# Attention on one Trainium2 core: queries and keys cast by the loading transfer, and 64-wide transposes in column tiles

## The chip, the cores and the metric

The kernel runs on one core of a Trainium2 chip. The time is the device time of one execution in microseconds (us), where lower is better. Several executions were timed of each version. The span is the length of one profiled execution on the chip, a little less than the timed one; the granted clock is the share of its full speed at which TensorE was let run. A run is called slow where it is over 1.5% above the fastest of the same kernel.

## The reference

```python
# q, k, v: float32, (batch 8, heads 8, seq 512, dim 64)
scale = 1.0 / np.sqrt(q.shape[-1])
scores = np.einsum('bhqd,bhkd->bhqk', q, k) * scale
scores = scores - scores.max(axis=-1, keepdims=True)
attn = np.exp(scores)
attn = attn / attn.sum(axis=-1, keepdims=True)
return np.einsum('bhqk,bhkd->bhqd', attn, v).astype(np.float32)
```

## The kernel before

The 64 heads are worked on as 32 pairs. A pair's queries and keys are loaded as fp32, cast to fp16, transposed on TensorE, and copied from PSUM by VectorE. TensorE then computes scores in blocks of 128 keys by 512 queries (a "unit", 256 in all), ScalarE takes the exponential of three units in one instruction, and TensorE multiplies by the values, with a column of ones for the sum. Eight units go through a polynomial on VectorE instead ("asides"). The order of all instructions is fixed when the kernel is built.

The parts that the change and the argument touch:

```python
def load(g, names="qkv"):                     # plain loads, on SyncE's queue
    ...
    for nm in names:
        r = lpool.tile([P, 2, NI * D], FP32, tag=f"{nm}32", name=f"{nm}32_{g}")   # 7 buffers a name
        nc.sync.dma_start(out=r, in_=rows(dict(q=q, k=k, v=v)[nm], g))
        raw[g, nm] = r

def cast_qk(g):                               # GpSimd: cast, and interleave the pair's two heads
    ...
    qk = xpool.tile([P, 2, NI, P], FP16, tag="qk", name=f"qk_{g}")
    for n in range(2):
        nc.gpsimd.tensor_copy(
            out=qk[:, n].rearrange("p i (h d) -> p i h d", d=D),
            in_=raw[g, "qk"[n]].rearrange("p h (i d) -> p i h d", d=D),
        )
    halves[g] = qk

def transpose(g, parts=(0, 1)):
    ...
    for n in parts:
        for i in range(NI):                   # 128-wide: both heads at once
            nc.tensor.transpose(ps[:, n - lo, i, :], halves[g][:, n, i, :], ident16)
    nc.vector.tensor_copy(out=turned[g][:, lo:hi], in_=ps)

# the opening
load_head(0, "q", nc.sync); load_head(0, "k", nc.scalar)      # pair 0 has its own path (both heads)
...
load(1, "qk")
load(0, "v")
for g in range(2, AHEAD):                     # AHEAD = 6
    load(g, "qk")
    load(g - 1, "v")
...
cast_qk(1); cast_v(0); cast_qk(2); cast_v(1)
# then, at the first unit of each pair g: cast_qk(g + 3), cast_v(g + 2), load(g + 6, "qk"), load(g + 5, "v")
```

The softmax here doesn't subtract the row's maximum and nothing guards it: scores larger than these inputs give would overflow.

## Time and profile before

| | before |
|---|---|
| median of the first three runs | 123.97 us (123.07 to 126.07) |
| profiled execution, span | 121.2 us |
| ScalarE busy | 113.9 us (94%) |
| exponentials: busy, and idle between them | 111.5 us, 0.8 us |
| GpSimd's casts of queries and keys | 62 instructions, 47.2 us |

The row to look at is ScalarE's. An engine that works without a pause from the opening to the close sets the end; the others matter only when they make it wait. The lines themselves are in the prediction.

### The profile page before, as it was taken

The numbers are of one execution on the slowest core, as the hardware profiler recorded it, in microseconds if no ns is written. First come the engines' busy times: TensorE is split into PE (matmuls) and PEld (weight loads), VectorE is DVE, ScalarE is ACT, GpSimd is POOL, SyncE is SP. The second block draws the span as 40 slices with busy tenths as digits, with TensorE's granted clock in tenths as the row PEclk, the third lists the DMA queues.
The fourth block names the chain that finished last, engine by engine and source line by source line (L and its number), as shares of the span: only waits on it lengthen the run. The fifth ranks groups of instructions, "written<-read, shape, count | busy, mean of one in ns | idle before, by whom it ended". The sixth has DMA issues, their size and how long they took to land.

```text
span 121.2 us, 4018 instructions
## 1 busy us (share of the span) xinstructions
PE 107.6 (89%) x1572; PEld 64.8 (53%) x1572; DVE 87.5 (72%) x213; ACT 113.9 (94%) x90; POOL 71.1 (59%) x109
## 2 busy tenths in 40 slices
PE   6989999898899998989988999899898998999680
PEld 6635646445564565456545656466455544666260
DVE  1342689979868985978787698766996899566170
ACT  4599999999999999999999999999999999999970
POOL 2188759869921992697199259990597099500000
PEclk9999999999999999999999999999999999999999
DMA  3999999999999999699999999999899895034213
GB/s 108 301 345 354 350 344 364 377 362 354 373 357 358 338 328 328 234 283 283 309 311 306 284 311 316 321 354 318 250 338 313 278 294 178 10 105 160 87 52 121
DMA packets 34882, 33.81 MB, mean 279 GB/s; under 512 B 2096, under 2 KB 34864, under 8 KB 34864
## 3 DMA queue, kind: packets, MB, share of 16 engines
q1 hardware_dynamic: 34576, 33.30, 84.6%
q10 hardware_dynamic: 288, 0.26, 0.7%
q8 instruction: 12, 0.20, 0.7%
q14 instruction: 6, 0.05, 0.1%
HBM read 25.17 MB, written 8.39 MB: 277 GB/s over the span
## 4 chain that ended last, share of the span: by engine, by line
ACT 74%; issue 15%; PE 5%; DMA 2%; DVE 1%
ACT pt L223 74%; DMA raw<-in_k_dram 2%; PE st L175 2%; PE o L234 1%; PE open L153 1%; DVE osb L248 1%; DVE rcp L247 0%; PE st L409 0%; DVE x L149 0%
## 5 line engine op out<-in xcount | busy, mean ns | idle before, releaser
L223 ACT ACTIVATE pt<-st 128x1536 f16<-128x1536 f32 (+2 forms) x85 | 111.5, 1609 | 0.8 <-PE st L175 0.8
L175 PE MATMUL st<-tqk 64*128 64x512 f16 x240 | 48.7, 380 | 7.0 <-ACT pt L223 5.9
L234 PEld LDWEIGHTS <-pt 128*128 128x128 f16 x992 | 33.8, 97 | 18.3 <-issue 12.4
L234 PE MATMUL o<-vp,pt 128*128 128x65 f16 x976 | 38.6, 194 | 0.9 <-DVE osb L248 0.3
L248 DVE TENSOR_TENSOR osb<-o,rcp 128x256 f32<-128x256 f32 x63 | 26.8, 425 | 2.2
L105 POOL CAST qk<-k 128x512 f16<-128x512 f32 x31 | 27.3, 880 | 0.6
L134 DVE COPY tqk<-tps 128x1024 f16<-128x1024 f16 (+1 forms) x32 | 21.2, 669 | 6.2 <-PE tps L133 5.9
L247 DVE RECIPROCAL rcp<-o 128x4 f32<-128x4 f32 x63 | 11.2, 178 | 17.4 <-PE o L234 17.1
L114 POOL CAST vp<-v 128x512 f16<-128x512 f32 x32 | 21.5, 672 | 2.6 <-DMA v<-in_v_dram 1.4
L105 POOL CAST qk<-q 128x512 f16<-128x512 f32 x31 | 19.9, 642 | 2.7 <-DMA q<-in_q_dram 1.8
L133 PEld LDWEIGHTS <-qk 128*128 128x128 f16 x248 | 14.2, 97 | 11.9 <-issue 4.5
L175 PEld LDWEIGHTS <-tqk 64*128 64x128 f16 x240 | 11.5, 93 | 15.8 <-issue 7.7
L133 PE MATMUL tps<-ident,qk 128*128 128x128 f16 x248 | 19.2, 220 | 0.7 <-DVE osb L248 0.3
L200 POOL TENSOR_SCALAR e<-n 128x512 int32<-128x512 int8 x8 | 5.0, 620 | 24.7 <-DVE n L197 24.6
L210 DVE SCALAR_TENSOR_TENSOR pa<-a,f 128x512 f16<-128x512 f32 x8 | 7.4, 930 | 0.0
L210 DVE SCALAR_TENSOR_TENSOR f<-f,e 128x512 f32<-128x512 f32 x8 | 6.9, 862 | 0.0
L210 DVE SCALAR_TENSOR_TENSOR a<-f 128x512 f32<-128x512 f32 x8 | 6.2, 771 | 0.0
L210 DVE SCALAR_TENSOR_TENSOR f<-sa,n 128x512 f32<-128x512 f32 x8 | 5.5, 692 | 0.3
L197 DVE TENSOR_SCALAR n<-sa 128x512 int8<-128x512 f32 x8 | 5.4, 681 | 0.0
L409 PE MATMUL warm<-blank 128*128 128x128 f16 x24 | 2.7, 313 | 1.0 <-DVE small L396 1.0
L234 PEld LDWEIGHTS <-pa 128*128 128x128 f16 x32 | 1.5, 97 | 3.6 <-DVE pa L210 1.7
L409 PEld LDWEIGHTS <-blank 128*128 128x128 f16 x28 | 2.7, 140 | 1.1 <-DVE small L396 1.0
(30 smaller groups left out, 20.4 us busy)
## 6 DMA issues: line engine op xcount, KB each, us to landing
v<-in_v_dram SPq DMA_DIRECT2D x32, 256.0 KB, 5.4
q<-in_q_dram SPq DMA_DIRECT2D x31, 256.0 KB, 5.1
k<-in_k_dram SPq DMA_DIRECT2D x31, 256.0 KB, 5.3
out_dram<-osb SPq DMA_DIRECT2D x31, 256.0 KB, 3.7
raw<-in_k_dram ACTq DMA_DIRECT2D x2, 128.0 KB, 2.9
raw<-in_q_dram SPq DMA_DIRECT2D x2, 128.0 KB, 2.7
out_dram<-osb SPq DMA_DIRECT2D x2, 128.0 KB, 1.7
```

Of the source, the lines that this page charges most:

```text
L105: nc.gpsimd.tensor_copy(out=qk[:, n].rearrange("p i (h d) -> p i h d", d=D), in_=raw[g, "qk"[n]].rearrange("p h (i d) -> p i h d", d=D),)
L114: nc.gpsimd.tensor_copy(out=vps[g % NV][:, :, :, 0:D], in_=raw[g, "v"].rearrange("p h (i d) -> p h i d", d=D),)
L133: nc.tensor.transpose(ps[:, n - lo, i, :], halves[g][:, n, i, :], ident16)
L134: nc.vector.tensor_copy(out=turned[g][:, lo:hi], in_=ps)
L175: nc.tensor.matmul(st[j][:, x, :], key, tq, start=True, stop=True)
L197: nc.vector.tensor_scalar(out=n, in0=s, scalar1=rate, scalar2=SHIFT, op0=AluOp.mult, op1=AluOp.add)
L210: nc.vector.scalar_tensor_tensor(out=o, in0=x, scalar=k, in1=y, op0=op0, op1=op1)
L223: nc.scalar.activation(out=pt[j][:, 0:n], in_=st[j][:, 0:n], func=EXP, scale=scale)
L234: nc.tensor.matmul(o[:, i, :], p[:, i * P : (i + 1) * P], vps[g % NV][:, h, c, :], start=(c == 0 and i == blocks[0]), stop=(c == NI - 1), ...
L247: nc.vector.reciprocal(out=rcp[:, lo:hi], in_=o[:, lo:hi, D:W])
L248: nc.vector.tensor_tensor(out=o_sb[g][:, h, lo:hi], in0=o[:, lo:hi, 0:D], in1=rcp[:, lo:hi].broadcast_to([P, hi - lo, D]), op=AluOp.mult,)
L409: nc.tensor.matmul(tile[:, G - 1, 0:P], blank, blank, start=True, stop=True)
```

## The change

Its intent is to take 47 us of casts from GpSimd. The transfer itself casts. The casting transfers are issued by GpSimd, so the loads of pairs 2 to 31 move from SyncE's queue to GpSimd's. Without a cast there is no interleave, so each head's 64 columns are transposed by themselves, into the upper or lower half of the PSUM tile's partitions.

```diff
+    def load_cast(g):
...
+        qk = xpool.tile([P, 2, 2, NI, D], FP16, tag="qk", name=f"qk_{g}", bufs=AHEAD + 4)
+        for n in range(2):
+            nc.gpsimd.dma_start(
+                out=qk[:, n].rearrange("p h i d -> p h (i d)"), in_=rows((q, k)[n], g)
+            )
+        halves[g] = qk
...
             for i in range(NI):
-                nc.tensor.transpose(ps[:, n - lo, i, :], halves[g][:, n, i, :], ident16)
+                for h in range(2):
+                    nc.tensor.transpose(
+                        ps[D * h : D * (h + 1), n - lo, i, :], halves[g][:, n, h, i, :], ident16
+                    )
...
         load(1, "qk")
-        load(0, "v")
-        for g in range(2, AHEAD):
-            load(g, "qk")
-            load(g - 1, "v")
+        for g in range(AHEAD - 1):
+            load(g, "v")
...
+        load_cast(2)
         cast_qk(1)
+        load_cast(3)
         cast_v(0)
-        cast_qk(2)
+        load_cast(4)
         cast_v(1)
+        load_cast(5)
...
-                        cast_qk(g + 3)
+                        load_cast(g + AHEAD)
                         cast_v(g + 2)
-                        load(g + AHEAD, "qk")
                         load(g + AHEAD - 1, "v")
```

Pair 1 is still loaded plainly and cast on GpSimd, without the interleave.

More of the change, by code (lines that the diff above doesn't have):

```diff
@@ L86, in load @@
             raw[g, nm] = r
+    def load_cast(g):
+        if g >= n_pairs:
+            return
+        qk = xpool.tile([P, 2, 2, NI, D], FP16, tag="qk", name=f"qk_{g}", bufs=AHEAD + 4)
[4 more added lines that the diff above has]
+        halves[g] = qk
     def load_head(h, nm, eng):
@@ L100, in cast_qk @@
     def cast_qk(g):
-        if g >= n_pairs:
-            return
-        qk = xpool.tile([P, 2, NI, P], FP16, tag="qk", name=f"qk_{g}")
+        qk = xpool.tile([P, 2, 2, NI, D], FP16, tag="qk", name=f"qk_{g}", bufs=AHEAD + 4)
         for n in range(2):
             nc.gpsimd.tensor_copy(
-                out=qk[:, n].rearrange("p i (h d) -> p i h d", d=D),
-                in_=raw[g, "qk"[n]].rearrange("p h (i d) -> p i h d", d=D),
+                out=qk[:, n].rearrange("p h i d -> p h (i d)"), in_=raw[g, "qk"[n]]
             )
```

## The prediction

> **What bounds the kernel now.** I read first the page's busy shares and slices, which say which engine could be the bound:
>
> ```profile
> PE 107.6 (89%) x1572; PEld 64.8 (53%) x1572; DVE 87.5 (72%) x213; ACT 113.9 (94%) x90; POOL 71.1 (59%) x109
> ...
> ACT  4599999999999999999999999999999999999970
> POOL 2188759869921992697199259990597099500000
> ...
> DMA  3999999999999999699999999999899895034213
> ```
>
> ScalarE (ACT) is at 9 tenths or more from the third slice to the last but one. GpSimd (POOL), from which the change takes work, is busy 59%. Second, the chain of work that ended last and the costliest groups, to see which operation this is and what it waits for:
>
> ```profile
> ACT 74%; issue 15%; PE 5%; DMA 2%; DVE 1%
> ...
> L223 ACT ACTIVATE pt<-st 128x1536 f16<-128x1536 f32 (+2 forms) x85 | 111.5, 1609 | 0.8 <-PE st L175 0.8
> L175 PE MATMUL st<-tqk 64*128 64x512 f16 x240 | 48.7, 380 | 7.0 <-ACT pt L223 5.9
> ...
> L105 POOL CAST qk<-k 128x512 f16<-128x512 f32 x31 | 27.3, 880 | 0.6
> ...
> L105 POOL CAST qk<-q 128x512 f16<-128x512 f32 x31 | 19.9, 642 | 2.7 <-DMA q<-in_q_dram 1.8
> ...
> L133 PE MATMUL tps<-ident,qk 128*128 128x128 f16 x248 | 19.2, 220 | 0.7 <-DVE osb L248 0.3
> ```
>
> The exponentials fill 111.5 of 121.2 us and were idle 0.8 us in all between them. The reader is to see that the rest is 121.2 - 111.5 - 0.8 = 8.9 us, which is the opening (the first exponential starts at 5.57 us in the timeline) and the close. No other part of this kernel can give more than the 0.8 us, unless it shortens the opening. No cast on GpSimd stands in the chain.
>
> Third, I looked at how much room TensorE has, since the change doubles the number of its transposes. This is the timeline of TensorE between 65.5 and 69.2 us (start, duration, engine, line, operation, count, idle before and its releaser):
>
> ```profile
> 65.78 0.59 PE L175 MATMUL st<-tqk 64*128 64x512 f16 x3 [0.16 <-ACT pt L223]
> 66.30 0.66 PE L234 MATMUL o<-vp,pt 128*128 128x65 f16 x16
> 66.80 0.61 PE L133 MATMUL tps<-ident,qk 128*128 128x128 f16 x8
> 67.34 0.60 PE L175 MATMUL st<-tqk 64*128 64x512 f16 x3
> 67.88 0.29 PE L234 MATMUL o<-vp,pa 128*128 128x65 f16 x4
> ```
>
> From start to start: three score matmuls 0.52 us, sixteen output matmuls 0.50, eight transposes 0.54 (before a score group). Only where a group has other tile shapes than the one ahead of it does it start at nearly the modelled end of that one; between output matmuls and transposes, both 128x128, there is no such gap.
>
> Fourth, the transfers over four stretches (busy us of PE, PEld, DVE, ACT, POOL, then clock, DMA share and GB/s), and the casts and preparations at the start:
>
> ```profile
> 20.00:40.00 20.00, 18.10 (x271) 10.62 (x269) 17.06 (x39) 20.00 (x17) 13.34 (x20) 1.00 1.08 365
> 40.00:60.00 20.00, 18.73 (x281) 11.12 (x279) 16.14 (x38) 20.00 (x17) 13.28 (x19) 1.00 0.93 295
> ...
> 5.83 0.62 POOL L105 CAST qk<-q 128x512 f16<-128x512 f32 x1 [1.26 <-DMA q<-in_q_dram]
> 6.59 0.62 POOL L105 CAST qk<-k 128x512 f16<-128x512 f32 x1
> ...
> 8.77 0.39 PE L175 MATMUL st<-tqk 64*128 64x512 f16 x2 [0.31 <-DVE tqk L134]
> ```
>
> The DMA queue can reach 365 GB/s and falls below it later, so it runs ahead of the need. At the start the chain is tight: the key cast of pair 1 ends at 7.21 us, and its first scores start at 8.77, released by the copy of its transposes. The exponentials around them start at 7.81 and 9.20, 1.39 us apart where the steady step is 1.33, so there the wait for pair 1 has just begun to show.
>
> **What the Trainium skill says.** (1) "DMA: Bandwidth & Descriptors", section "Latency and other measured facts": a transfer issued from GpSimd has a first byte after about 1 us, which the page puts down to the emission of descriptors by the engine's cores, against 0.6 us from the hardware queues. The kernel before issues all loads and stores from SyncE and two from ScalarE, so no row of its trace shows this. (2) "TensorEngine Tiling (Array Packing)", sections "Key Properties" and "Restrictions": a change of tiling mode drains TensorE, different tiles can load weights and multiply in parallel, and column tiling disables Fast Weight Load. The timeline agrees with the drain, as just read; for row tiles it agrees with the parallelism: three 512-column score matmuls have a group time of 0.60 us where one alone lasts 0.38. The opening has 64-wide transposes already (128*64), but all of one head into one column half; they took 0.63 us for eight, hardly more than the 0.62 of eight 128-wide ones, so a lone 64-wide transpose costs as much as a whole one. (3) "TensorE: Matmul & The Clock Gate", Part 3: three column tiles at 512 columns ran 2.38 times as fast as one after the other. At 128 columns with a weight load for each no run here shows it. (4) "SBUF - State Buffer", section "Who interferes with whom": VectorE in a two-port mode shuts GpSimd out of SBUF and so delays its descriptors, while an instruction with at most one SBUF input and no such mode doesn't. Here nearly all of VectorE's work reads PSUM (copies of transposes, normalisation), so I count on little of that.
>
> **The change part by part.**
>
> GpSimd. Removed: 30 pairs' casts of queries and keys, 30 x (0.642 + 0.880) = 46 us of busy time (pair 1 keeps its cast, pair 0 has its own opening). Added: 60 transfers issued by GpSimd. With the skill's 1 us as my estimate for one, 60 us. Per pair, GpSimd then has 2 x 1.0 + 0.67 (value cast) + a quarter of 0.62 (the aside's step) = 2.8 us. ScalarE needs per pair 248 units / 32 / 3 x 1.333 = 3.44 us. So GpSimd still keeps up, with an 18% margin. On the path: 0.
>
> DMA. Bytes read from HBM stay the same and bytes written to SBUF fall. A pair moves 4 x 256 KB = 1.05 MB: 2.9 us at 365 GB/s against 3.44. Hidden, unless casting makes it slower.
>
> TensorE. 8 transposes of a pair become 16 of half the width, the same 128 columns streamed by each. If the two heads' column tiles run side by side: 8 x 0.056 = 0.45 us as now ((0.61 - 0.22) / 7 = 0.056 for each further one). If one after the other: 16 x 0.059 = 0.94 (0.059 from the opening's eight, in the same way). The third tile mode adds a drain next to output matmuls, my estimate 0.1 us a pair (a score matmul group to an output group: 0.52 us in place of about 0.43 for two passes of 0.21). TensorE's need per pair now: scores 2.58 x 0.52 = 1.34, outputs 2 x 0.50 = 1.00, transposes 0.45, drains ahead of the scores 2.58 x 0.1 = 0.26, aside 0.05; sum 3.10 against 3.44. It becomes 3.2 (parallel) or 3.7 (serial). I choose parallel as the likelier because row tiles visibly do it.
>
> VectorE: its copies of the turned tiles are unchanged, 0.69 us each. Its asides may gain a little without GpSimd's casts beside them, off the path.
>
> The opening. This is the part that I expect to see. GpSimd's order is now: load of pair 2 (two transfers), then the cast of pair 1. The transfers can only be issued after GpSimd's part of the opening (4.23 + 0.34 = 4.57 us), so the cast of pair 1 starts at 4.57 + 2 x 1.0 = 6.6 rather than at 5.83: 0.7 us later. As read above there is hardly any slack from that cast to the exponential at 9.20, so about 0.6 of it goes into the end time. Pair 2's own data come only by about 9.6 (6.6, and some 3 us for 512 KB at half the bandwidth beside the value loads); its transposes are queued at 9.1, ahead of scores needed by 10.5. With everything moved by 0.6 that costs another 0 to 0.5; I put 0.3. The steady part: 0, with 0.1 for a few late turns.
>
> Sum: + 0.6 + 0.3 + 0.1 = + 1.0 us on 123.97, so 125.0 us.
>
> **The rivals.**
>
> Column tiles run one after the other. TensorE then needs 3.7 us a pair and takes the bound from ScalarE: 30 x (3.7 - 3.44) = + 8, about 132 us. For it: a weight load for each of 16 short transposes, without the fast load. Against it: row tiles overlap, and the skill's column figure. Halfway (0.7 us for the sixteen) it is 3.45 us a pair, and costs 1 to 2.
>
> The casting transfer is slower than the plain one. Of a pair's 2.9 us, queries and keys take half, 1.46; they may stretch by 3.44 - 2.9 = 0.54 us, 37%, before DMA sets the pace. At half speed it would be 4.4 us a pair: + 0.9 x 30, less a lead of up to six pairs, some + 15 to 25. Against it: half the bytes to write. Nothing in this trace measures it.
>
> Issuing takes 1.5 us or more. GpSimd would need 3.8 us a pair and fall behind by 10 us in the whole; the lead of six pairs (20 us) hides most, but the value casts lag. The opening would cost 1 us more: 126 to 130.
>
> The opposite: the early plain queue carries less, so values and pair 1 land sooner, and the order costs nothing; 123.5. A gain over 2% would need 2.5 us out of ScalarE's 0.8 us of waits and an opening that no edit shortens: next to nothing.
>
> **Range and chances.** The three runs before lie between 123.07 and 126.07, so the low end is 123.4. The upper end must hold the half-serial TensorE and a slow issue, and touch the serial case: 131. I give serial or half-serial enough to hurt 0.17, slow casting transfers 0.09, slow issue or late casts 0.07: slower 0.33. Faster 0.03. The rest, 0.64, is within 2%.
>
> **What would show it.** Right: the 64-wide transposes of a pair take 0.45 to 0.55 us; the exponential's idle time is 1 to 2 us and lies before 15 us of the span; GpSimd's issues last about 1 us; steps of 1.333 us between exponentials later. Wrong: score matmuls that no longer wait for ScalarE, and gaps between exponentials in every pair (serial tiles); transposes released by transfers in mid-kernel (slow casting); GpSimd busy throughout and output matmuls waiting for value casts (slow issue). The prediction falls if ScalarE's idle time in the steady part exceeds 2 us, or if the cast of pair 1 isn't late.

## The result, and the profile after

The changed kernel took 128.89 us (median of 4 runs, 127.69 to 129.08); the kernel before, in the same rounds and earlier, 124.94 us (4 runs, 123.07 to 126.07, the two longest slow). The ratio of the fast runs is 1.0414, 95% interval 1.0289 to 1.054: slower. Ratios here and below are the mean time of one kernel's fast runs over the mean of the other's fast runs of the same rounds, so they are not quite the ratio of the medians quoted.

The page of the changed kernel, its lines on the same groups as shown of before:

```profile
PE 111.5 (88%) x1820; PEld 67.5 (53%) x1820; DVE 85.8 (68%) x213; ACT 114.3 (90%) x90; POOL 70.8 (56%) x109
...
ACT  4683399999999999999999999999999999999940
...
PEclk9996579999999999999999999999999999999859
...
L233 ACT ACTIVATE pt<-st 128x1536 f16<-128x1536 f32 (+2 forms) x85 | 111.9, 1541 | 5.9 <-PE st L185 5.8
...
L141 PE MATMUL tps<-ident,qk 128*64 128x128 f16 x496 | 20.4, 225 | 4.1 <-DMA qk<-in_q_dram 2.6
...
L93 POOL DMA_DIRECT2D qk<-in_q_dram x30 | 22.2, 739 | 0.4
L93 POOL DMA_DIRECT2D qk<-in_k_dram x30 | 21.8, 728 | 0.0
```

The row of the clock in the kernel before, for comparison:

```profile
PEclk9999999999999999999999999999999999999999
```

The exponentials are as long as before but idle 5.9 us instead of 0.8, and the second row says where: in slices 4 and 5, at the start. The third row has TensorE's clock falling there and once more at the end. GpSimd's casts are gone, and 44 us of issuing transfers have come in their place.

The chain of waits in the changed kernel names the reason (start, duration, what):

```profile
4.60 0.82 POOL qk L93
5.43 7.73 DMA qk<-in_k_dram
13.20 0.64 PE tps L141 x5
13.84 1.40 PE st L185 x6
15.23 1.87 PE o L244 x32
17.10 0.78 PE st L185 x3
17.90 1.12 ACT pt L233
```

The keys of pair 2 are 7.73 us on their way. Their transposes, the scores after them and so the exponentials stand until 13.2 us. Before, pair 2's transposes began at 9.1 us:

```profile
9.10 0.78 PE L133 MATMUL tps<-ident,qk 128*128 128x128 f16 x8
```

Pair 1's first cast, at 5.83 us in the prediction's lines, starts at 6.35:

```profile
6.35 0.61 POOL L113 CAST qk<-q 128x512 f16<-128x512 f32 x1 [0.20 <-DMA q<-in_q_dram]
```

Where the 5.9 us of span between these two executions went (the fast runs differ by 5.1 us in the mean) can be read from two marks in the chain of waits: the start of the ninth exponential, and the end of the last exponential that stands in the chain (two more of three units follow it off the chain). First before, then after:

```profile
14.54 1.14 ACT pt L223
112.42 1.68 ACT pt L223
```

```profile
19.25 1.46 ACT pt L233
117.21 1.67 ACT pt L233
```

| | before | after | difference |
|---|---|---|---|
| start to ninth exponential | 14.54 | 19.25 | + 4.71 |
| ninth exponential to end of the last one in the chain | 99.56 | 99.63 | + 0.07 |
| from there to the end | 7.1 | 8.2 | + 1.1 |

So the steady part is untouched. All that was lost was lost in the opening and the close.

In the steady part the sixteen narrow transposes of a pair take no longer than the eight wide ones (TensorE's timeline of the changed kernel):

```profile
60.33 0.67 PE L244 MATMUL o<-vp,pt 128*128 128x65 f16 x16
60.92 0.64 PE L141 MATMUL tps<-ident,qk 128*64 128x128 f16 x16
61.49 0.60 PE L185 MATMUL st<-tqk 64*128 64x512 f16 x3
```

Start to start they take 0.57 us, against 0.54 for the eight wide ones at 66.80 in the prediction's timeline.

### The profile page after: what moved, and what is told of

The parts are those of the page before. It is cut to its first block, busy times and chain, and to the rows that moved or that the text cites.

```text
span 127.1 us, 4402 instructions
## 1 busy us (share of the span) xinstructions
PE 111.5 (88%) x1820; PEld 67.5 (53%) x1820; DVE 85.8 (68%) x213; ACT 114.3 (90%) x90; POOL 70.8 (56%) x109
## 3 DMA queue, kind: packets, MB, share of 16 engines
q0 software_dynamic: 16320, 7.87, 49.7%
## 4 chain that ended last, share of the span: by engine, by line
ACT 64%; issue 16%; DMA 8%; PE 7%; POOL 1%; DVE 0%; ACTq 0%
ACT pt L233 64%; DMA qk<-in_k_dram 6%; PE o L244 4%; PE st L185 3%; DMA raw<-in_k_dram 2%; POOL qk L93 1%; PE o_last L244 1%; PE tps L141 1%; DVE osb L258 0%; ACTq L102 0%; POOL x L159 0%; DVE rcp L257 0%
## 5 line engine op out<-in xcount | busy, mean ns | idle before, releaser
L185 PE MATMUL st<-tqk 64*128 64x512 f16 x240 | 49.5, 389 | 5.8 <-ACT pt L233 5.0
L244 PEld LDWEIGHTS <-pt 128*128 128x128 f16 x992 | 35.3, 100 | 19.4 <-issue 10.5
L244 PE MATMUL o<-vp,pt 128*128 128x65 f16 x976 | 40.4, 198 | 1.1 <-DVE osb L258 0.5
L144 DVE COPY tqk<-tps 128x1024 f16<-128x1024 f16 (+1 forms) x32 | 21.3, 670 | 11.7 <-PE tps L141 11.2
L121 POOL CAST vp<-v 128x512 f16<-128x512 f32 x32 | 22.1, 692 | 5.0 <-PE o L244 4.9
L141 PE MATMUL tps<-ident,qk 128*64 128x128 f16 x496 | 20.4, 225 | 4.1 <-DMA qk<-in_q_dram 2.6
L141 PEld LDWEIGHTS <-qk 128*64 128x64 f16 x496 | 15.5, 111 | 15.8 <-issue 8.9
L93 POOL DMA_DIRECT2D qk<-in_q_dram x30 | 22.2, 739 | 0.4
L93 POOL DMA_DIRECT2D qk<-in_k_dram x30 | 21.8, 728 | 0.0
L220 DVE SCALAR_TENSOR_TENSOR pa<-a,f 128x512 f16<-128x512 f32 x8 | 6.1, 767 | 0.0
L220 DVE SCALAR_TENSOR_TENSOR f<-f,e 128x512 f32<-128x512 f32 x8 | 5.5, 681 | 0.0
```

Of the source, the lines that this page charges most:

```text
L93: nc.gpsimd.dma_start(out=qk[:, n].rearrange("p h i d -> p h (i d)"), in_=rows((q, k)[n], g))
L121: nc.gpsimd.tensor_copy(out=vps[g % NV][:, :, :, 0:D], in_=raw[g, "v"].rearrange("p h (i d) -> p h i d", d=D),)
L141: nc.tensor.transpose(ps[D * h : D * (h + 1), n - lo, i, :], halves[g][:, n, h, i, :], ident16)
L185: nc.tensor.matmul(st[j][:, x, :], key, tq, start=True, stop=True)
L220: nc.vector.scalar_tensor_tensor(out=o, in0=x, scalar=k, in1=y, op0=op0, op1=op1)
L244: nc.tensor.matmul(o[:, i, :], p[:, i * P : (i + 1) * P], vps[g % NV][:, h, c, :], start=(c == 0 and i == blocks[0]), stop=(c == NI - 1), ...
```

## The experiments

Each was timed in the same rounds as the kernel before and on the same chip as it (the batches ran on four different chips). My theory: pair 2's transfers are late because of the seven value loads on the shared transfer engines (SyncE issued them from 2.63 to 6.31 us, four of them ahead of pair 2's first load at 4.55); the rivals were the late issue on GpSimd, slow casting, and the narrow transposes.

**e1_tiles: the transposes alone.** The kernel before, with plain loads and casts on GpSimd, but without the interleave:

```diff
-                out=qk[:, n].rearrange("p i (h d) -> p i h d", d=D),
-                in_=raw[g, "qk"[n]].rearrange("p h (i d) -> p i h d", d=D),
+                out=qk[:, n].rearrange("p h i d -> p h (i d)"), in_=raw[g, "qk"[n]]
   # and the transposes as in the changed kernel
```

> Only the 64-wide transposes in column tiles, on the kernel before: queries and keys are still loaded plainly by SyncE and cast on GpSimd, without the interleave. If the loss comes from the order of the first transfers (my theory), this kernel is as fast as the one before: ratio 0.99 to 1.01, sixteen transposes in about 0.64 us, exponentials idle under 1.5 us. If the narrow transposes cost something (rival): ratio over 1.02 and gaps between exponentials in the steady part.

Measured: 123.87 us against 123.39, ratio 1.0021 (0.9972 to 1.007), exponentials idle 1.0 us. The narrow transposes cost nothing that this shows.

**e3_held: fewer value loads ahead.** The changed kernel with one number changed:

```diff
-            r = lpool.tile([P, 2, NI * D], FP32, tag=f"{nm}32", name=f"{nm}32_{g}")
+            r = lpool.tile([P, 2, NI * D], FP32, tag=f"{nm}32", name=f"{nm}32_{g}",
+                           bufs=3 if nm == "v" else AHEAD + 1)
```

> The changed kernel, with 3 buffers for the raw values rather than 7, so that the fourth value load must wait for GpSimd's cast of the first (about 9 us): only three value loads are queued when pair 2's casting loads are issued, at the same time as before (4.55 and 5.43 us). If the queue of earlier transfers is what delays them (my theory), pair 2's keys land by about 9.5 us rather than 13.2 and the idle time of the exponentials falls to 1 to 2.5 us: ratio to the kernel before 1.00 to 1.02. If the late issue on GpSimd or slow casting is the cause (rivals), the keys still land after 12 us and the ratio stays at about 1.04.

Measured: 125.13 us, ratio 1.0075 (1.0017 to 1.0132). Pair 2's casting loads, issued at the same times as in the changed kernel (4.55 and 5.44 us), now take 4.6 and 4.8 us from issue to landing instead of 7.1 and 7.7, so the keys land at 10.2 us, 0.7 later than I had put. The exponentials are idle 3.4 us, more than I expected; that profile fell in an execution whose opening matmuls ran at half speed until about 13 us (its sixteen transposes of pair 2 took 1.06 us, later ones 0.64), so its idle time is not comparable with the others'. Pair 2's transposes started at 11.76 us there and waited for no transfer; by these times an opening at full speed, which came to them at 9.1 us before, would still have waited for the keys. The ratio is the mean of the two other fast runs (124.59 and 124.00 us).

What the two queues moved says how pair 2 was held up (the view of the transfers; q0 is GpSimd's queue, q1 SyncE's; packets, MB, share of 16 engines). First the changed kernel from 5 to 8 us, then from 9 to 12:

```profile
q1 hardware_dynamic: 1016, 0.98, 96.2%
```

```profile
q1 hardware_dynamic: 592, 0.57, 66.0%
q0 software_dynamic: 492, 0.24, 58.4%
```

Then e3_held, from 8 to 9 us:

```profile
q0 software_dynamic: 375, 0.18, 136.7%
q1 hardware_dynamic: 24, 0.02, 5.7%
```

In the changed kernel not one packet of GpSimd's queue ran in the three microseconds after the first issue had begun at 4.55 and ended at 5.4; its first 14 came between 8 and 9 us (the first at 8.5, 4.0 us after the issue began). Then the two queues shared about evenly. The Trainium skill, "DMA: Bandwidth & Descriptors", section "Queues, rings and completion order", says that each engine takes turns between the queues with work; the second stretch agrees (592 to 492 packets), the first doesn't. Only part of that silence is the usual start: where later issues of the changed kernel found this queue empty or nearly so (at 23.27 and 44.51 us), the first packets came 1.5 us after the issue began, though the plain queue was busy then too. In the opening it was 4.0 us here, 3.3 in e3_held and 2.3 in e2_early below. With only three value loads ahead, GpSimd's queue had the engines nearly to itself from 8 us.

The same fence removes a rival. Alone, the casting queue did 375 packets in 1 us. One issue is 272 packets for 256 rows of 1 KB, so as fp32 read it is about 375 x 256 / 272 x 1,024 B = 361 KB in 1 us, an estimate of 360 GB/s: as much as the plain queue moved, loads and stores, from 20 to 40 us before (365). A casting packet holds its engine longer (49.7% x 16 x 127.1 us / 16320 = 62 ns on the page of the changed kernel, against 84.6% x 16 x 121.2 / 34576 = 47 ns for the plain ones before), but they overlap, which the share over 100% shows.

**e11_held5: a dose between**, with five value buffers (one look, no timing).

> A dose between: 5 value buffers (7 in the changed kernel, 3 in the held one). If the plain loads queued earlier are what pair 2 waits for, its loads take between 4.7 us (held) and 7.4 us (changed) from issue to landing: about 6. If what mattered in the held kernel was something else, such as a free SyncE: 4.7 or 7.4.

Measured: 6.4 and 6.6 us from issue to landing, between 4.7 (three buffers) and 7.4 (seven), first packets again between 8 and 9 us (13 of them). So the landing follows the number of plain loads, though the first packets came no earlier with five than with seven. The single time, 125.85 us, decides nothing.

**e8_uncast: the queue without the cast** (one look): the same transfers on GpSimd's queue, fp32 to fp32, cast by VectorE ahead of the transposes.

> A look, not a candidate: the same loads on GpSimd's queue without casting (fp32 to fp32), with the cast on VectorE ahead of the transposes. It is to show whether the delay of pair 2 comes with the queue or with the cast. If with the queue (my theory), the first packets again appear only about 8 to 9 us, pair 2 lands after 12 us, and each issue takes about 0.72 us. If casting is what is slow (rival), pair 2 lands about 9.5 us. The packets of this queue should take about 48 ns of an engine each as on SyncE's queue, where the casting ones took 62. VectorE will be overloaded, so the kernel as a whole will be slower than 1.05.

Measured: pair 2's transfers take 6.8 and 6.9 us to land (the keys at about 12.4), and GpSimd's queue again moved nothing until the stretch from 8 to 9 us (9 packets). So in this one execution the delay comes without the cast as well. The issues took 0.72 us. My figure for the packets was wrong: they are larger here (4,800 for 15.73 MB), 162 ns each, so they can't be compared with 48. At 178 us the kernel is overloaded on VectorE, as meant.

**e2_early: pair 2 issued first.** The changed kernel, with `load_cast(2)` moved from the end of the opening to just ahead of `load(1, "qk")`.

> The changed kernel, with the casting load of pair 2 issued as GpSimd's first transfer, right after the identity matrix (about 1.3 us rather than 4.55). If pair 2 is late because its loads join a queue behind seven value loads, they now land before 8 us, the exponentials' idle time falls from 5.9 us to under 2, and the ratio to the kernel before is 0.99 to 1.015. If casting transfers are slow by themselves (rival), they still take over 6 us to land, and the ratio stays over 1.02.

Measured: 125.53 us, ratio 1.0148 (1.0082 to 1.0214), exponentials idle 2.5 us. Issued at 1.44 and 2.33 us, the transfers still took 6.1 to 6.8 us and landed at about 8.3, a little over my 8, but in time. Two more of my figures were missed: the idle time isn't under 2 us, and over 6 us to land was what I had set as the rival's sign, so this run alone doesn't clear the cast; that takes e8_uncast and the 375 packets in 1 us. The cost has moved: GpSimd's timeline shows pair 1 waiting for its data, and TensorE's shows pair 3 doing so.

```profile
6.98 0.61 POOL L113 CAST qk<-q 128x512 f16<-128x512 f32 x1 [2.44 <-DMA q<-in_q_dram]
7.97 0.61 POOL L113 CAST qk<-k 128x512 f16<-128x512 f32 x1 [0.38 <-DMA k<-in_k_dram]
```

```profile
14.36 0.41 PE L141 MATMUL tps<-ident,qk 128*64 128x128 f16 x8 [0.63 <-DMA qk<-in_q_dram]
15.01 0.41 PE L141 MATMUL tps<-ident,qk 128*64 128x128 f16 x8 [0.24 <-DMA qk<-in_k_dram]
```

The late issue was thus part of the cause, but issuing early only passes the wait on while the values still stand in the way.

**e5_both and e12_both5: both edits.** `load_cast(2)` first and three value buffers; the second run is the same kernel with more rounds.

> The changed kernel with both edits that helped singly: pair 2's casting load issued as GpSimd's first, and 3 value buffers. Issued early, it took pair 1's bandwidth (pair 1's query cast began at 6.98 us rather than 5.83) and pair 3 then stood behind the values (14.36). If queueing for the 16 engines explains all, pair 3 is now in time and only pair 1's 1.1 us stay: ratio to the kernel before 1.005 to 1.012. If something else in the steady part costs time (rival), it stays at 1.015 as with the early issue alone.

> The kernel with both edits (early casting load of pair 2, 3 value buffers) again, with more rounds, since its interval reached from 0.992 to 1.021. My theory, with pair 1's later data as the only loss left: ratio to the kernel before 1.004 to 1.012. A loss in the steady part would put it over 1.015; a gain from the freed GpSimd under 1.0.

Measured: 124.35 us against 124.72, ratio 1.0064 (0.9918 to 1.0209), and then 125.71 against 123.75, ratio 1.007 (1.0032 to 1.0108). What is left is the gap that I named: the fifth exponential of the first of these profiles starts at 10.74 us after 1.44 us idle, waiting for pair 1. No wait lies in the steady part. (The second profile fell in an opening at half speed until 13 us, like e3_held's, so its waits aren't compared.)

**e6_warm: the clock.** The changed kernel, with 48 dummy matmuls ahead of pair 2's transposes, so that TensorE works while it waits:

```diff
+        if g == 2:
+            keep = aux([P, S], FP32, "keep")
+            for _ in range(48):
+                nc.tensor.matmul(keep[:, 0:P], blank, blank, start=True, stop=True)
         ps = aux([P, hi - lo, NI, P], FP16, f"tps_{g}_{lo}")
```

> The changed kernel, with 48 dummy matmuls ahead of pair 2's transposes, so that TensorE isn't idle while it waits (9.1 to 11.7 us). Pair 2 is as late as in the changed kernel, but if half of the loss after its landing is the halved clock, the granted clock now stays at 1.0 between 10 and 18 us, the 0.28 us gap at 17.9 goes, the exponential after the stall starts about 14.2 rather than 14.84 us, and the ratio falls from 1.04 to 1.025 to 1.035. If the clock is of no account: ratio unchanged at 1.04.

Measured: 126.56 us against 124.72, ratio 1.0252 (1.0165 to 1.034), at the lower end of what I gave. Pair 2's data come no earlier: the first half of its transposes starts at 11.72 us, the second at 13.26 (11.70 and 13.20 without the dummies). This is the stretch from 10 to 20 us in the changed kernel and then in e6_warm (busy us of PE, PEld, DVE, ACT, POOL, then granted clock, DMA share, GB/s):

```profile
10.00:20.00 10.00, 7.44 (x110) 4.63 (x110) 2.96 (x8) 5.45 (x5) 9.06 (x14) 0.66 1.38 216
```

```profile
10.00:20.00 10.00, 8.46 (x162) 5.96 (x159) 3.71 (x11) 6.25 (x6) 8.82 (x14) 1.00 1.37 223
```

The clock stays at 1.00 instead of 0.66. The exponential after the stall starts at 14.25 rather than 14.84 us, the later gap of 0.28 us is gone, and the ninth starts at 18.26 rather than 19.25: 1.0 us. The close is shorter as well: from the end of the last exponential in the chain (116.14 + 1.66) to the end of the span (124.7) it is 6.9 us, against 8.2 in the changed kernel. In these two lines of the closes, the changed kernel's first, the sixteen output matmuls take 1.06 us where they take 0.66 in the chain of e6_warm:

```profile
121.87 1.06 PE L244 MATMUL o<-vp,pt 128*128 128x65 f16 x16
```

```profile
120.07 0.66 PE o L248 x16
```

**e7_order: the old order of the opening**, with pair 2 loaded plainly and cast on GpSimd as before, three value buffers, and casting loads from pair 3 on.

> The opening of the kernel before, in its order (pair 1, values 0, pair 2 plainly, cast on GpSimd), with 3 value buffers, and pair 3's casting load as GpSimd's first; all later pairs by casting loads. My theory: ratio to the kernel before 0.995 to 1.008, exponentials idle about 1 us. If the steady part with casting loads costs anything: over 1.01.

Measured: 125.44 us against 124.72, ratio 1.0052 (0.9865 to 1.0239), unclear. Only two of its four runs were fast (123.23 and 124.96 us), and its profile fell in a slow one, so it agrees with the theory and proves little.

**e4_plain2: a failed try at the same.** Pair 2 loaded plainly right after pair 1 (ahead of all values), but with GpSimd's cast of the first values ahead of the cast of pair 2.

> The changed kernel, with pair 2 loaded plainly by SyncE right after pair 1 and cast on GpSimd, as pair 1 is; casting loads start with pair 3. My theory says that all of the loss lies in pair 2's arrival: ratio to the kernel before 0.99 to 1.01, idle time of the exponentials about 1 us. If casting loads cost in the steady part too (rival), a loss of 1% or more remains.

Measured: 127.13 us, ratio 1.0286 (1.0226 to 1.0347). The mistake was mine. GpSimd's instructions ran in program order, and it stood 2.12 us for values that were now loaded behind pair 2; pair 2's cast began only at 9.76 us and pair 3's casting loads at 10.88, so pair 3 was late too (its transposes waited at 14.90). It tests another order, not the theory.

**e9_before11 and e10_order11: using a GpSimd free of casts.** Eleven units on VectorE instead of eight, in the kernel before and in e7_order:

```diff
-    aside = [(g, 0, 0) for g in (3, 6, 10, 13, 16, 19, 23, 26)]
+    aside = [(g, 0, 0) for g in (3, 5, 8, 11, 13, 16, 18, 21, 23, 26, 28)]
```

> The kernel before with 11 rather than 8 of the 256 exponential units computed on VectorE, a control for the next run. ScalarE has 3 x 0.427 = 1.3 us less to do; VectorE 3 x about 3.6 us more (5 passes of 0.68 to 0.93), to about 82% busy, beside GpSimd's casts. Ratio to the kernel before: 0.985 to 1.005.

> The kernel with the order of the opening restored (casting loads from pair 3 on, 3 value buffers), with the same 11 units on VectorE. Its passes are shorter without GpSimd's casts beside them (0.767 rather than 0.930 us for the last one in the changed kernel's profile). If the freed GpSimd is worth anything, this is the version that beats both: ratio 0.985 to 0.995. If the opening sets all, it is the same as the control.

Measured: ratios 1.0406 (1.0346 to 1.0467) and 1.0543 (1.0481 to 1.0606). Both expectations missed, and the kernel with casting loads is the slower of the two. The profiles (e9_before11's of a slow run) show waits of the exponentials for output matmuls in mid-kernel (3.1 us and 4.0 us in all) that the kernel before has none of. The fixed order of this kernel was laid out for eight; I didn't look for one that fits eleven. No version that I ran beats the kernel before.

## Why the prediction was right or wrong

The measured time lies in the range given (123.4 to 131.0), but well above the 125.0 named, and slower had been given 0.33, for causes that did not come. Of the two costs that it named for the opening, one was no cost and the other over ten times as large; the clock was not in it. The exponentials' idle time was to be 1 to 2 us and was 5.9. That the time lies in the range at all is luck: the upper end had been set for serial transposes and a slow issue.

- **The bound.** Right. ScalarE sets the pace before and after, and taking 47 us of casts from GpSimd bought nothing. Its busy time hardly fell either (71.1 to 70.8 us), since 44 us of issuing came in their place.
- **Column tiles side by side.** Right. In the trace of pair 1 the two heads' transposes start in pairs (7.32 and 7.32 us, 7.40 and 7.40). (0.64 - 0.22) / 15 = 0.028 us for each further narrow transpose, so about 0.45 us for sixteen, and e1_tiles at 1.0021. The serial rival falls.
- **Casting transfers hidden in the steady part.** Right. The steady part grew by 0.07 us in 99.6, and the casting queue alone reached an estimated 360 GB/s of reads. That rival falls.
- **GpSimd keeps up.** Right, with room: an issue takes 0.72 us in the median (0.71 to 0.89 in all 60, so no sign that VectorE delays them), not the 1.0 estimated. That 1.0 was the skill's time to a first byte, which is another thing than GpSimd's time for an issue.
- **"the cast of pair 1 starts at 4.57 + 2 x 1.0 = 6.6 rather than at 5.83"**, worth 0.6. Wrong. The cast was late, by 0.5 us, and not only by the issues, which ended at 6.15; it then waited 0.20 us for its own data. But it cost nothing: pair 1's first scores started at 8.68 us, not later than the 8.77 of before. What failed is the reading "hardly any slack". In the kernel before, the key cast ended at 7.21 us and the first transpose of keys started at 7.76, behind other work of TensorE; in the changed kernel they stand at 7.69 and 7.74. So about 0.5 us had been free, and the delay used it up.
- **"Pair 2's own data come only by about 9.6"**, worth 0.3. This is the term that was mis-sized. The keys came at 13.2. I had let them share the bandwidth evenly from the moment of issue, so 3 us for 512 KB. The trace shows no packet of that queue before 8.5 us and an even share only after about 9, beside seven plain value loads. Three of them instead of seven bring the keys at 10.2 us (e3_held), so 3.0 of the 3.6 us by which I was off belong to these loads; e11_held5 lies between, and e8_uncast has the delay without the cast. In e6_warm, where the clock plays no part, this delay is worth 18.26 - 14.54 = 3.7 us.
- **The clock.** Not in the prediction at all. TensorE, idle from about 9.1 to 11.7 us, fell to half its clock at about 10.7 (0.71 on average from 10.5 to 11) and stayed there until about 17.5. e6_warm puts this at 19.25 - 18.26 = 1.0 us in the opening. The close ran at half clock too, 1.1 us more than before. Sum: 3.7 + 1.0 + 0.1 + 1.1 = 5.9 us, the difference of the spans.

Two things stay open. Why the close lost its clock: TensorE's waits there look the same in the kernels that kept it, the changed kernel's four timed runs have a mean clock of 0.957 to 0.966 and e6_warm's four 0.994 to 1.000, and I have no run that moves the close alone. It may not be in every run: in the shortest of the four (span 125.9 us, mean clock 0.966) I estimate 8.6 us at half clock from these two figures, where the others have 10.4 to 10.9, and its span is 1.2 us shorter. And why GpSimd's queue got nothing for the first 4.0 us, rather than the 1.5 of later issues: that the engines had already been handed the plain queue's rows would fit, but no run shows it.

## What to carry to other kernels

When a load moves to another queue, look first at what is already queued on the shared transfer engines at that moment: raw bandwidth and a fair share don't tell when a transfer lands that is issued among seven others. The first transfers of a kernel deserve their own plan, since no lead covers them; hold back whatever isn't needed soon by giving it fewer buffers. And a wait of TensorE can cost more than its length, because the clock may be halved for several microseconds after it.

## What the Trainium skill lacked or had wrong

- "DMA: Bandwidth & Descriptors", on turns between queues: with a backlog on SyncE's queue, GpSimd's queue moved 0 packets in the 2.6 us after its first issue had ended at 5.4 us, and shared evenly (592 to 492 packets) from 9 us on. The page doesn't tell of such a start.
- The same page, first byte after about 1 us for a transfer issued from GpSimd: here the first packets ran 1.5 us after the start of an issue in mid-kernel, but 2.3 us (e2_early), 3.3 us (e3_held) and 4.0 us (the changed kernel) after it in the opening. The issue itself took 0.72 us on GpSimd for 256 rows of 1 KB, a figure that the page lacks.
- The same page gives no rate for casting loads: 375 packets in 1 us, an estimated 360 GB/s of fp32 read, with a single packet at 62 ns against 47 plain.
- "TensorEngine Tiling (Array Packing)" has no measurement for short transposes in column tiles: sixteen 64-wide ones in two column tiles took 0.64 us, eight 128-wide ones 0.61, weight loads included.
- "TensorE: Matmul & The Clock Gate", Part 1, puts the fall to half clock after at least one idle window of about 3.4 us. Here the granted clock fell at about 10.7 us, 1.6 us after TensorE's last matmul had ended at 9.07, and stayed at half some 7 us (0.66 on average from 10 to 20 us). And in executions that began with half-speed matmuls (sixteen transposes in 1.06 us in e3_held's opening) the profile's clock still read 1.00, so that row doesn't show a slow start; the page warns only in general that clock events in a trace can be unreliable.
